# A one-core encoder layer in fp32: squares moved between engines at the start, SSD chunk outputs ahead of the next chunk, embedding product behind its gate

## The chip, the cores and the metric

The kernel runs on one core of a Trainium2 chip. The metric is device time in microseconds of one execution. The five engines are PE (TensorE, matmuls), DVE (VectorE), ACT (ScalarE), POOL (GpSimd) and SP (SyncE, which issues the DMAs here, strictly in order).

## The reference

One layer of a hybrid streaming encoder, for 512 prompt tokens and 32 sample tokens (T = 544 together), width 1024:

```
h = rmsnorm(x); q, k, v, z, xBC, dt, gates = split(h @ w_in)
ya = band_attention(rms(q), rms(k), v, rel_bias)          # 16 heads of 64, chunk band of 9 x 64 tokens
xs, B, C = split(silu(causal_dwconv(xBC)))                # 32 heads of 64 in 4 groups, state 128
y = chunked scan: per chunk  (C B^T * decay) @ (dt x) + C @ h * exp(acs);  h' = h * exp(last) + B^T @ wj
yb = rmsnorm((y + d_skip * xs) * silu(z))
x += (sigmoid(ga) * (ya @ w_proj_a) + sigmoid(gb) * (yb @ w_proj_b)) @ w_out
x += down(gelu(conv(ug)) * conv(uv))                      # u = rmsnorm(x) @ w_up
x += sigmoid(rmsnorm(x) @ w_ple_gate) * (p @ w_ple)
```

Outputs are x and the new caches and states. The sample tokens go through the same code with their own cached context.

## The kernel before

Activations lie transposed, 128 features by 544 tokens, in eight tiles. Every dense product is made from fp32 split into a high and a low part (`hi`, `lo` for activations, `wh`, `wl` for weights): `mm3` (L283) issues `wh*hi`, `wh*lo` and `wl*hi`, each for two halves of 272 tokens. This group of six matmuls is called a chunk below; a dense step has eight chunks (an embedding step `pw` only two) and ends with an epilogue that takes the result out of one of two PSUM buffers `dps`. The weights come as raw units of 128x1024 (`wr`, two per DMA, two DMAs' worth of buffers), are cast on ACT (L250) and their low part is made on DVE or, for odd early units, on POOL (L254).

The order of all dense steps is a list, `dense_steps` (L31). `dense.run(n)` works off n chunks of it, and the code of the other stages is written between such calls: this is what places SSD scan, attention and statistics between the dense matmuls on PE. The tile framework schedules each engine's instructions from this program order and puts in the semaphores; on an engine they then run in that order.

- **Beginning.** `Dense.start` (L334) runs the first two steps together while x is still arriving: `split_g` (L371) makes `hi` on ACT (L374) and `lo` on DVE (L375) for x[0] to x[7]. The squares of x are made on POOL for k = 0 to 3 (L443, added L445), on ACT for 4 to 7 (L380, L383), and summed on DVE (L384, L448) into `acc`. `rstd_of` (L392) multiplies `acc` by ones on PE (`rps`) and takes Ln (L404) and Exp (L409) on ACT. The `dt` product (`dtp`, L473) follows. Until `rstd` is there no epilogue can run.
- **Bias table.** `bias_vector` (L551) negates a small table (`er`, L554), copies it (`e0`, L555), writes both to DRAM (`evec`, L556, L557), from where 16 DMAs (`bsc`, L563, 320 KB each) spread it.
- **SSD scan** (loop L1139). Four groups of heads, in each the prompt chunks 0 to 3 and the sample chunk 4, which goes together with chunk 0 (a pair): 16 turns. `ssd_a` (L613) makes `cbt` and the transposes `xst` on PE, scales `dx` and `wj` on DVE (L637), loads `ab` by DMA (L645), and from it makes the decay `m` (relu L650, exp L655 on ACT, product L656 on DVE) and the scaled C (exp L659 on ACT, product L660 on POOL). `ssd_b` (L665) multiplies (`yps`), adds the outputs to `xs` on DVE (L690), makes the new state (`st` on PE, POOL L699, DVE L701, or an ACT copy L703 for chunk 0), and writes `out_o_hs` (L705) after chunk 4 and `out_o_hp` (L710) after chunk 3. A turn is `ssd_a(n)`, some dense chunks, `ssd_b(n-1)`, some dense chunks. `cbt`, `xst`, `yps` and `st` share four PSUM slots.
- **Attention.** Eight pairs of heads in blocks of 128 queries. `stack` (L816) prepares the keys and queries `ks`, `qs` of the next pair, `att_a` makes the logits `L`, `att_b` transposes the weights (`Tp`), `att_c` multiplies by v. `FILL` (L1157) holds for each block how many dense chunks stand before and behind `att_b`.
- **End.** After the last `down` step come eight `pw` steps, copied to SBUF by ACT (L1089), a second `rstd`, eight gate steps with tanh (`ep_final`, L1096), the last of them in two halves (`last_gate`, L1104).

## Time and profile before

| | |
|---|---|
| median of 3 runs (lowest, highest) | 1356.16 us (1355.61, 1357.16) |
| profiled execution | 1355.77 us |
| its span | 1354.1 us |
| mean granted clock of PE over the span | 0.999 |
| PE busy | 1338.2 us, 99% |
| DVE, ACT, POOL busy | 852.6, 634.4, 313.7 us |
| DMA | 142.15 MB, 106 GB/s over the span |

The span is the profiled part of the execution; the remaining 1.67 us lie around it. Busy times of engines overlap. In timelines, consecutive instructions of one kind are one row, whose duration goes from the first start to the last end.

### The profile page before, as it was taken

Reading aid. Unit: us, or ns where it says so; the run is one execution under the profiler, and the core shown is the slowest. Engines: PE = TensorE matmul, PEld = TensorE weight load, DVE = VectorE, ACT = ScalarE, POOL = GpSimd, SP = SyncE. Lnnn points to the kernel's source line nnn. Section 1 sums busy time; section 2 is a strip of 40 time slices with the busy share of each in tenths; the row PEclk is TensorE's granted clock in tenths of the full one; section 3 lists DMA queues with packets and bytes.
Section 4 is the critical chain, followed back from the end, with each engine's and each line's share of the span. In section 5 each row is a group of like instructions: output and inputs, shape, how many; then the busy total and the mean of one; then the engine's idle time right before and its main releaser. Section 6 shows DMA issues by size and latency. Waiting matters only on the chain.

```text
span 1354.1 us, 26563 instructions
## 1 busy us (share of the span) xinstructions
PE 1338.2 (99%) x11045; PEld 1307.2 (97%) x11045; DVE 852.6 (63%) x1474; ACT 634.4 (47%) x1104; POOL 313.7 (23%) x442
## 2 busy tenths in 40 slices
PE   8999999999999999999999999999999999999998
PEld 7999998999999999999999999999999999999998
DVE  7999889755775656643554335677676356753545
ACT  5465555656676667542442223534444124432342
POOL 5456365544321211100000000133332013310000
PEclk9999999999999999999999999999999999999999
DMA  5733243332533332222223422222222232222231
GB/s 182 252 100 130 83 128 121 119 132 100 177 94 114 115 111 90 67 81 94 69 89 110 143 94 73 85 94 94 94 72 85 94 111 94 76 85 94 94 107 53
DMA packets 41896, 142.15 MB, mean 105 GB/s; under 512 B 9216, under 2 KB 13232, under 8 KB 29488
## 3 DMA queue, kind: packets, MB, share of 16 engines
q1 hardware_dynamic: 41776, 140.45, 31.4%
q8 instruction: 87, 1.43, 0.4%
q14 instruction: 33, 0.27, 0.1%
HBM read 129.27 MB, written 14.31 MB: 106 GB/s over the span
## 4 chain that ended last, share of the span: by engine, by line
PE 89%; DVE 6%; ACT 2%; DMA 1%; issue 1%; SPq 0%; POOL 0%; ACTq 0%; DVEq 0%; POOLq 0%
PE dps L130 80%; PE O L130 2%; PE yps L130 2%; PE L L130 1%; PE st L130 1%; DVE cv L599 1%; DVE qs L834 1%; PE Tp L133 1%; DVE wl L254 1%; PE xst L133 0%; PE gps L130 0%; DMA wr<-in_w 0%; DVE xs L603 0%; DMA ab<-asc 0%; PE qn L130 0%
## 5 line engine op out<-in xcount | busy, mean ns | idle before, releaser
L130 PE MATMUL dps<-hi,wh 128*128 128x272 f32 x2960 | 627.0, 293 | 0.6 <-DVE ext L574 0.4
L130 PE MATMUL dps<-lo,wh 128*128 128x272 f32 x2960 | 613.1, 288 | 4.1 <-DVE lo L375 4.1
L130 PE MATMUL dps<-hi,wl 128*128 128x272 f32 x2960 | 612.1, 288 | 0.0
L130 PEld LDWEIGHTS dps<-hi,wh 128*128 128x128 f32 x2960 | 466.0, 189 | 10.5 <-issue 7.8
L130 PEld LDWEIGHTS dps<-lo,wh 128*128 128x128 f32 x2960 | 465.9, 189 | 5.0 <-DVE lo L375 5.0
L130 PEld LDWEIGHTS dps<-hi,wl 128*128 128x128 f32 x2960 | 464.9, 188 | 0.0
L250 ACT CAST wh<-wr 128x1024 fp32r<-128x1024 f32 x192 | 201.2, 1048 | 386.0 <-PE dps L130 346.6
L254 DVE TENSOR_TENSOR wl<-wr,wh 128x1024 fp32r<-128x1024 f32 x173 | 213.6, 1235 | 47.6 <-ACT wh L250 42.3
L1033 DVE SCALAR_TENSOR_TENSOR ucv<-uext,vec,ucv 128x546 f32<-128x546 f32 x96 | 75.3, 784 | 4.4 <-ACT ucv L1030 2.7
L599 DVE SCALAR_TENSOR_TENSOR cv<-ext,hv,cv 128x547 f32<-128x547 f32 x72 | 71.0, 986 | 2.1 <-ACT cv L596 1.0
L1026 POOL COPY cfo<-uext 128x2 f32<-128x2 f32 x48 | 10.4, 217 | 261.7 <-DVE uext L573 261.7
L1023 POOL MEMSET uext<- 128x2 f32 x48 | 4.5, 95 | 278.7 <-issue 278.7
L1065 DVE TENSOR_TENSOR x<-x,dps 128x544 f32<-128x544 f32 x24 | 17.3, 721 | 78.0 <-PE dps L130 78.0
L571 DVE TENSOR_TENSOR uext<-dps,rstd 128x272 f32<-128x272 f32 x48 | 21.3, 443 | 63.0 <-PE dps L130 58.3
L785 DVE CUSTOM_DVE_ANT_0 P<-L,bias 128x128 f32<-128x128 f32 (+3 forms) x64 | 30.8, 481 | 46.1 <-PE L L130 41.6
L254 POOL TENSOR_TENSOR wl<-wr,wh 128x1024 fp32r<-128x1024 f32 x19 | 48.4, 2549 | 43.9 <-ACT wh L250 42.4
L1027 POOL COPY cfo<-uext 128x2 f32<-128x2 f32 x48 | 55.5, 1157 | 0.0
L787 ACT ACTIVATE P<-P,sm 128x128 f32<-128x128 f32 (+3 forms) x64 | 36.0, 562 | 26.8 <-DVE sm L785 26.4
L660 POOL TENSOR_TENSOR ab<-ab,bc 128x512 f32<-128x512 f32 (+1 forms) x28 | 37.0, 1325 | 40.7 <-ACT ab L659 40.7
L368 ACT CAST hi<-me 128x544 fp32r<-128x544 f32 x24 | 15.5, 647 | 61.9 <-DVE me L1051 61.9
L1030 ACT ACTIVATE ucv<-uext,vec 128x546 f32<-128x546 f32 x48 | 40.7, 847 | 7.2 <-DVE uext L574 2.6
L650 ACT ACTIVATE m<-ab,tm 128x128 f32<-128x128 f32 x128 | 40.8, 389 | 6.3 <-DMA ab<-asc 6.2
(243 smaller groups left out, 1548.9 us busy)
## 6 DMA issues: line engine op xcount, KB each, us to landing
wr<-in_w SPq DMA_DIRECT2D x96, 1024.0 KB, 4.9
ab<-asc SPq DMA_DIRECT2D x32, 256.0 KB, 5.1
bsc<-evec SPq DMA_DIRECT2D x16, 320.0 KB, 8.0
bias<-bsc SPq DMA_DIRECT2D x16, 256.0 KB, 3.2
xin<-in_xT SPq DMA_DIRECT2D x8, 272.0 KB, 5.7
out_o_v<-v SPq DMA_DIRECT2D x8, 272.0 KB, 3.2
out_o_k<-qk SPq DMA_DIRECT2D x8, 272.0 KB, 2.9
x<-in_xT SPq DMA_DIRECT2D x8, 272.0 KB, 4.4
```

Source lines behind the costliest of these rows:

```text
L130: return self._pin(nc.tensor.matmul(*args, **kw))
L250: cp = S.copy(hi, r)
L254: eng.tensor_tensor(lo, r, hi.bitcast(F32), op=SUB)
L571: V.tensor_tensor(ext[:, n : n + HALF], ps[:, 0, :HALF], rstd[:, 0:HALF], op=MUL)
L599: V.scalar_tensor_tensor(y[:, :n], ext[:, j : j + n], hv[:, 24 * j + ti : 24 * j + ti + 1], y[:, :n], op0=MUL, op1=ADD)
L650: S.activation(m[:, i], ab[:Q, i], AF.Relu, scale=-1.0, bias=tm[:Q, 1, c, hd : hd + 1])
L660: G.tensor_tensor(ab, ab, cc[:, tk].unsqueeze(1).to_broadcast([128, H, Q]), op=MUL)
L785: V.tensor_tensor_reduce(out=P, in0=L, in1=B, scale=1.0, scalar=3e38, op0=ADD, op1=MIN, accum_out=nm[:n])
L787: S.activation(P, P, AF.Exp, scale=-1.0, bias=nm[:n], accum_out=sm[:n])
L1027: G.tensor_copy(cfo[:, i, 2:4], ext[:, UW - 2 : UW])
L1030: S.activation(y[:, :n], ext[:, 0:n], AF.Identity, scale=vec[:, V_FW + i : V_FW + i + 1], bias=vec[:, V_FB + i : V_FB + i + 1])
L1033: V.scalar_tensor_tensor(y[:, :n], ext[:, j : j + n], vec[:, V_FW + 48 * j + i : V_FW + 48 * j + i + 1], y[:, :n], op0=MUL, op1=ADD)
```

## The change

- The squares at the beginning: x[0] on ACT directly into `acc` behind the first weight parts, x[1] to x[5] on ACT behind the last split, x[6] and x[7] on POOL with their sum; DVE adds the six results behind the last `lo`. The load of `hb` goes out before that of the second weight pair.
- The `dt` product is cut in two halves, one before and one behind the statistics matmul.
- The table's negate is tied behind the last instruction of the dt softplus (`last_dt`), the copy follows it.
- In `rstd_of`, Ln and Exp stand in one loop.
- SSD: `ssd_b(n-1)` directly ahead of `ssd_a(n)`, then all dense chunks of the turn.
- `FILL`: block (even pair, 2) from (2, 3) to (3, 4), block (even pair, 3) from (2, 4) to (2, 2).
- End: gate steps first, the statistics six chunks behind the last `down`, tanh kept in eight tiles, then the `pw` steps, whose result DVE reads from PSUM; the last `pw` step in two halves.

```diff
-    p += [("pw", m) for m in range(8)] + [("gate", m) for m in range(8)]
+    p += [("gate", m) for m in range(8)] + [("pw", m) for m in range(8)]
...
+            dtp = [dt_product(0)]
             first_rstd.append(rstd_of(rstd, acc, 1.0 / D))
+            dtp.append(dt_product(1))
             for st, ps in zip(sts, pss):
                 epilogue[st[0]](ps, *st[1:])
-            dt_product()
+            dt_scale(dtp)
...
             ln = S.activation(dst[:, sl], ps[:, :HALF], AF.Ln, bias=eps, scale=scale)
...
-        for h in range(2):
-            sl = slice(h * HALF, (h + 1) * HALF)
             last = S.activation(dst[:, sl], dst[:, sl], AF.Exp, scale=-0.5)
...
+        if k == 0:
+            sq0 = S.activation(acc, xt[0], AF.Square)
+            tc.add_manual_dep(sq0.ins, last_part[0].ins.name, ORDER, reason="order")
+    nc.sync.dma_start(hb, a["hb"].unsqueeze(0).to_broadcast([128, 2, 32]))
     load(1)
-    nc.sync.dma_start(hb, a["hb"].unsqueeze(0).to_broadcast([128, 2, 32]))
...
-    acc2 = slot(name="acc2")
-    for k in range(KD):
-        if k < 4:
-            q = acc2 if k == 0 else eslot("sq")[:, :T]
-            G.tensor_tensor(q, xt[k], xt[k], op=MUL)
-            if k > 0:
-                G.tensor_tensor(acc2, acc2, q, op=ADD)
-        else:
-            if k == 6:
-                V.tensor_tensor(acc, acc, acc2, op=ADD)
-            add_sq(acc, xt[k], k == 4, V)
-    done(acc2)
+    q6, q7 = eslot("sq"), eslot("sq")
+    for q, k in ((q6, 6), (q7, 7)):
+        G.tensor_tensor(q[:, :T], xt[k], xt[k], op=MUL)
+    G.tensor_tensor(q6[:, :T], q6[:, :T], q7[:, :T], op=ADD)
+    for k in range(1, 6):
+        q = eslot("sq")
+        tc.add_manual_dep(S.activation(q[:, :T], xt[k], AF.Square).ins, last_split[0].ins.name, ORDER, reason="order")
+        tc.add_manual_dep(V.tensor_tensor(acc, acc, q[:, :T], op=ADD).ins, last_split[1].ins.name, ORDER,
+                          reason="order")
+    V.tensor_tensor(acc, acc, q6[:, :T], op=ADD)
...
-        V.tensor_scalar(er[0:16, 0:257], er[0:16, 0:257], -1.0, None, op0=MUL)
+        neg = V.tensor_scalar(er[0:16, 0:257], er[0:16, 0:257], -1.0, None, op0=MUL)
+        tc.add_manual_dep(neg.ins, last_dt[0].ins.name, ORDER, reason="order")
...
+            if m == 7:
+                sp2 = sum_parts(acc)
+                dense.defer(6, lambda: rstd_of(rstd, sp2, 1.0 / D, gelus))
...
     def ep_pw(ps, m):
-        t = slot(name="pw")
-        S.copy(h2(t), pv(ps))
-        pw.append(t)
...
+        t = pg[m]
+        V.scalar_tensor_tensor(h2(t), h2(t), 1.0, pv(ps), op0=ADD, op1=MUL)
+        V.scalar_tensor_tensor(x[m], t, 0.5, x[m], op0=MUL, op1=ADD)
         nc.sync.dma_start(a["o_y"][m], x[m])
...
-        nxt = [ssd_a(g, i) for i in ((4, 0), (1,), (2,), (3,))[c]]
-        fa, fb = ((10, 9), (8, 8), (8, 7), (8, 7))[c]
-        dense.run(fa)
         if prev is not None:
             ssd_b(prev)
-        prev = nxt
-        dense.run(fb)
+        prev = [ssd_a(g, i) for i in ((4, 0), (1,), (2,), (3,))[c]]
+        dense.run((19, 16, 15, 15)[c])
...
-    FILL = {(0, -1): (2, 2), (0, 0): (3, 1), (0, 1): (1, 3), (0, 2): (2, 3), (0, 3): (2, 4),
+    FILL = {(0, -1): (2, 2), (0, 0): (3, 1), (0, 1): (1, 3), (0, 2): (3, 4), (0, 3): (2, 2),
...
-    last_gate()
+    last_pw()
```

On DVE, at the beginning, behind the first three `lo`, the kernel before has (L375 is `lo`, L384 and L448 the additions of squares, `hv` small scalings of constants):

```order
L375 SCALAR_TENSOR_TENSOR lo<-xin,vec,hi 128x544 x3
L384 TENSOR_TENSOR acc<-acc,sq 128x544
L459 TENSOR_SCALAR hv<-vec 128x120
L460 TENSOR_SCALAR hv<-vec 128x16
L461 TENSOR_SCALAR hv<-vec 128x1
L375 SCALAR_TENSOR_TENSOR lo<-xin,vec,hi 128x544
L448 TENSOR_TENSOR acc<-acc,acc_200 128x544
L375 SCALAR_TENSOR_TENSOR lo<-xin,vec,hi 128x544
L384 TENSOR_TENSOR acc<-acc,sq 128x544 x2
L254 TENSOR_TENSOR wl<-wr,wh 128x1024
```

and the changed kernel (L380 is `lo`, L452 and L454 the additions):

```order
L380 SCALAR_TENSOR_TENSOR lo<-xin,vec,hi 128x544 x4
L463 TENSOR_SCALAR hv<-vec 128x120
L464 TENSOR_SCALAR hv<-vec 128x16
L465 TENSOR_SCALAR hv<-vec 128x1
L380 SCALAR_TENSOR_TENSOR lo<-xin,vec,hi 128x544
L452 TENSOR_TENSOR acc<-acc,sq 128x544 x5
L454 TENSOR_TENSOR acc<-acc,sq 128x544
L255 TENSOR_TENSOR wl<-wr,wh 128x1024
```

Four additions became six, and all stand behind the last `lo`. On SP, from the last copies of the bias table to the loads of the second SSD chunk, the kernel before has:

```order
L563 DMA bsc_254<-evec 128x640
L237 DMA wr<-in_w 128x2048 x2
L545 DMA asc<-dtx 32x4x128
L547 DMA asc<-dtx 32x32
L237 DMA wr<-in_w 128x2048
L645 DMA ab<-asc 128x8x32
L645 DMA ab<-asc 128x512 x2
L237 DMA wr<-in_w 128x2048
L645 DMA ab<-asc 128x512 x2
L237 DMA wr<-in_w 128x2048
L705 DMA out_o_hs<-h 128x512
L645 DMA ab<-asc 128x512 x2
```

and the changed kernel, where nine of the 16 `bsc` come behind `asc`:

```order
L553 DMA asc<-dtx 32x4x128
L555 DMA asc<-dtx 32x32
...
L572 DMA bsc_254<-evec 128x640
L238 DMA wr<-in_w 128x2048
L654 DMA ab<-asc 128x8x32
L654 DMA ab<-asc 128x512 x2
L238 DMA wr<-in_w 128x2048
L714 DMA out_o_hs<-h 128x512
L654 DMA ab<-asc 128x512 x2
L238 DMA wr<-in_w 128x2048
L654 DMA ab<-asc 128x512 x2
```

The `bsc` moved from ahead of two weight loads to directly ahead of the first `ab`, and the second pair of `ab` (chunk 1) from ahead of `out_o_hs` to behind it; the same exchange is found in all four groups. On DVE, at the first pair of the scan, the kernel before has (`m` of 32x256 is chunk 4, the two of 128x512 are chunk 0):

```order
L656 TENSOR_TENSOR m<-m,cbt 32x256
L599 SCALAR_TENSOR_TENSOR cv<-ext,hv,cv 128x547 x2
L656 TENSOR_TENSOR m<-m,cbt 128x512
L571 TENSOR_TENSOR ext<-dps,rstd 128x272
L573 TENSOR_TENSOR ext<-dps,rstd 128x240
L574 TENSOR_TENSOR ext<-dps,rstd 128x32
L603 SCALAR_TENSOR_TENSOR xs<-th,cv 128x512
L604 SCALAR_TENSOR_TENSOR xs<-th,cv 128x32
L656 TENSOR_TENSOR m<-m,cbt 128x512
```

and the changed kernel (L699 are the additions of the outputs, which read `yps`):

```order
L665 TENSOR_TENSOR m<-m,cbt 32x256
L608 SCALAR_TENSOR_TENSOR cv<-ext,hv,cv 128x547
L665 TENSOR_TENSOR m<-m,cbt 128x512
L580 TENSOR_TENSOR ext<-dps,rstd 128x272
L582 TENSOR_TENSOR ext<-dps,rstd 128x240
L583 TENSOR_TENSOR ext<-dps,rstd 128x32
L255 TENSOR_TENSOR wl<-wr,wh 128x1024
L699 SCALAR_TENSOR_TENSOR xs<-xs,vec,yps 128x32
L612 SCALAR_TENSOR_TENSOR xs<-th,cv 128x512
L613 SCALAR_TENSOR_TENSOR xs<-th,cv 128x32
L699 SCALAR_TENSOR_TENSOR xs<-xs,vec,yps 128x32 x3
L665 TENSOR_TENSOR m<-m,cbt 128x512
```

The second `m` of chunk 0 moved behind the output additions of chunk 4.

## Rows read from the trace of the kernel before

**Rows 1.** The page, part 1: busy us (share of the span) and instructions of each engine.

```profile
PE 1338.2 (99%) x11045; PEld 1307.2 (97%) x11045; DVE 852.6 (63%) x1474; ACT 634.4 (47%) x1104; POOL 313.7 (23%) x442
```

**Rows 2.** Waits of PE: waiting line <- releaser: us in total, times, longest.

```profile
PE dps L130 <- DVE lo L375: 4.1, 3, 3.3
PE st L130 <- DVE xs L690: 1.8, 2, 1.2
...
PE L L130 <- DMA ks<-ks: 1.0, 2, 0.8
...
PE L L130 <- ACT qs L752: 0.6, 1, 0.6
```

**Rows 3.** Windows: us, busy (instructions) of PE, PEld, DVE, ACT, POOL, clock, DMA.

```profile
0.00:20.00 20.00, 14.42 (x73) 13.05 (x74) 13.63 (x19) 11.68 (x20) 14.59 (x28) 0.91 0.89 301
...
80.00:160.00 80.00, 79.34 (x689) 75.06 (x688) 76.70 (x138) 48.67 (x102) 41.10 (x53) 1.00 0.35 111
...
600.00:620.00 20.00, 20.00 (x162) 20.00 (x161) 7.53 (x8) 7.34 (x8) 0.00 (x0) 1.00 0.32 106
```

**Rows 4.** Timeline of PE, beginning: start, duration, operation, count [idle before <- releaser].

```profile
16.15 0.55 PE L130 MATMUL dps<-lo,wh 128*128 128x272 f32 x2 [3.27 <-DVE lo L375]
...
25.07 1.08 PE L130 MATMUL rps<-acc,ones 128*128 128x272 f32 x4
...
28.56 0.49 PE L130 MATMUL dps<-hi,wh 128*128 128x272 f32 x2 [0.44 <-DVE ext L574]
```

**Rows 5.** Timeline of DVE, beginning.

```profile
10.97 3.35 DVE L260 TENSOR_TENSOR wl<-wr,wh 128x512 fp32r<-128x512 f32 x2
14.24 4.70 DVE L375 SCALAR_TENSOR_TENSOR lo<-xin,vec,hi 128x544 fp32r<-128x544 f32 x3
...
21.80 1.54 DVE L384 TENSOR_TENSOR acc<-acc,sq 128x544 f32<-128x544 f32 x2
```

**Rows 6.** Timeline of POOL, beginning.

```profile
10.43 1.84 POOL L445 TENSOR_TENSOR acc<-acc,sq 128x544 f32<-128x544 f32 x1
```

**Rows 7.** Timeline of DVE: the copy of the bias table and the last dt step.

```profile
28.34 2.58 DVE L555 COPY e<-er 16x383 f32<-16x383 f32 x1
...
55.52 0.31 DVE L512 SCALAR_TENSOR_TENSOR tm<-dtt 128x160 f32<-128x160 f32 x1
```

**Rows 8.** Timeline of SP's DMA issues, 30 to 102 us.

```profile
32.48 1.21 SPq L563 DMA_DIRECT2D bsc<-evec  x2
...
34.38 14.32 SPq L563 DMA_DIRECT2D bsc<-evec  x14
...
72.86 1.53 SPq L645 DMA_DIRECT2D ab<-asc  x3
...
101.91 0.34 SPq L705 DMA_DIRECT2D out_o_hs<-h  x1
```

**Rows 9.** The page, part 6: DMA issues, KB each, median us from issue to landing.

```profile
ab<-asc SPq DMA_DIRECT2D x32, 256.0 KB, 5.1
bsc<-evec SPq DMA_DIRECT2D x16, 320.0 KB, 8.0
bias<-bsc SPq DMA_DIRECT2D x16, 256.0 KB, 3.2
```

**Rows 10.** Timeline of PE: outputs of the first pair.

```profile
95.81 0.65 PE L130 MATMUL yps<-m,dx 32*64 32x32 f32 x16
```

**Rows 11.** Timeline of DVE: the second product of chunk 0 of the first group.

```profile
87.87 0.67 DVE L656 TENSOR_TENSOR m<-m,cbt 128x512 f32<-128x512 f32 x1
```

**Rows 12.** Timelines of ACT and POOL: from the first relu to the last product, chunk 1.

```profile
92.90 1.28 ACT L650 ACTIVATE m<-ab,tm 128x128 f32<-128x128 f32 x4 [0.28 <-DMA ab<-asc]
...
101.20 1.29 POOL L660 TENSOR_TENSOR ab<-ab,bc 128x512 f32<-128x512 f32 x1
```

**Rows 13.** Timeline of DVE at the last `down` step.

```profile
1288.42 0.72 DVE L1065 TENSOR_TENSOR x<-x,dps 128x544 f32<-128x544 f32 x1 [2.58 <-PE dps L130]
...
1292.70 0.73 DVE L389 TENSOR_TENSOR al<-acc,ah 128x544 fp32r<-128x544 f32 x1 [0.84 <-ACT ah L388]
```

More of the change, by code (lines that the diff above doesn't have):

```diff
@@ L228, in trunk @@
     raws = {0: r0}
+    last_part = []
     ready = {}
@@ L258, in prep_part @@
         hi, lo = ready[u]
-        S.copy(hi[:, c0:c1], r[:, c0:c1])
+        last_part[:] = [S.copy(hi[:, c0:c1], r[:, c0:c1])]
         V.tensor_tensor(lo[:, c0:c1], r[:, c0:c1], hi[:, c0:c1].bitcast(F32), op=SUB)
@@ L370, in split @@
         return hi, lo
+    last_split = []
     def split_g(x, g):
         hi, lo = slot(F32R, "hi"), slot(F32R, "lo")
-        S.activation(hi, x, AF.Copy, scale=g)
-        V.scalar_tensor_tensor(lo, x, g, hi.bitcast(F32), op0=MUL, op1=SUB)
+        last_split[:] = [S.activation(hi, x, AF.Copy, scale=g),
+                         V.scalar_tensor_tensor(lo, x, g, hi.bitcast(F32), op0=MUL, op1=SUB)]
         return hi, lo
@@ L471, in trunk, with dt_product, dt_scale @@
     bsc = [dram.tile([128, EROW], F32, name=f"bsc{h}", tag=f"bsc{h}") for h in range(16)]
-    def dt_product():
-        ps = [sps("dtp") for _ in range(2)]
-        for h in range(2):
-            for k in range(KD):
-                j = 32 * (k % 4)
-                PE.matmul(ps[h][j : j + 32, :HALF], lhsT=dtw[:, 32 * k : 32 * k + 32],
-                          rhs=xt[k][:, h * HALF : (h + 1) * HALF], start=k < 4, stop=k >= 4)
+    def dt_product(h):
+        ps = sps("dtp")
+        for k in range(KD):
+            j = 32 * (k % 4)
+            PE.matmul(ps[j : j + 32, :HALF], lhsT=dtw[:, 32 * k : 32 * k + 32],
+                      rhs=xt[k][:, h * HALF : (h + 1) * HALF], start=k < 4, stop=k >= 4)
+        return ps
+    last_dt = []
+    def dt_scale(ps):
         done(dtw_t, *xt)
@@ L511, in dt_softplus @@
         dt = tm[:, 0]
-        V.scalar_tensor_tensor(dt, p, 2.0, x, op0=MUL, op1=ADD)
+        last_dt.append(V.scalar_tensor_tensor(dt, p, 2.0, x, op0=MUL, op1=ADD))
         ea = const.tile([128, 32], F32, name="ea")
@@ L1075, in trunk @@
     ph = []
-    pw = []
+    pg = []
     def acts_pw(st):
@@ L1083, in acts_pw, with ep_final_gate @@
         return ph
-    parts = []
-    def ep_pw(ps, m):
-        t = slot(name="pw")
-        S.copy(h2(t), pv(ps))
-        pw.append(t)
-        if m == 0:
-            parts.append(sum_parts(acc))
-        if m == 7:
-            dense.defer(4, lambda: rstd_of(rstd, parts[0], 1.0 / D, gelus))
-    def ep_final(ps, m):
-        t = eslot("pg")
-        V.tensor_tensor(h2(t[:, :T]), pv(ps), h2(rstd), op=MUL)
-        S.activation(t[:, :T], t[:, :T], AF.Tanh, scale=0.5)
-        V.scalar_tensor_tensor(t[:, :T], t[:, :T], 1.0, pw[m], op0=ADD, op1=MUL)
-        V.scalar_tensor_tensor(x[m], t[:, :T], 0.5, x[m], op0=MUL, op1=ADD)
+    def ep_final_gate(ps, m):
+        t = slot(name="pg")
+        V.tensor_tensor(h2(t), pv(ps), h2(rstd), op=MUL)
+        S.activation(t, t, AF.Tanh, scale=0.5)
+        pg.append(t)
@@ L1102, in ep_final, with last_pw @@
+    def ep_pw(ps, m):
+        t = pg[m]
+        V.scalar_tensor_tensor(h2(t), h2(t), 1.0, pv(ps), op0=ADD, op1=MUL)
+        V.scalar_tensor_tensor(x[m], t, 0.5, x[m], op0=MUL, op1=ADD)
         nc.sync.dma_start(a["o_y"][m], x[m])
-    def last_gate():
-        t, m = eslot("pg"), 7
+    def last_pw():
+        m = 7
+        t = pg[m]
         pss = [sps("gps") for _ in range(2)]
-        w = next_unit(*units_of(("gate", m))[0])
+        ws = [tuple(w[:, 768 + 128 * j : 896 + 128 * j] for w in pw_w["w"]) for j in range(2)]
@@ L1108, in last_gate @@
         for h in range(2):
             sl = slice(h * HALF, (h + 1) * HALF)
-            for n in range(KD):
-                wh, wl = (v[:, 128 * n : 128 * n + 128] for v in w)
-                for i, (l, r) in enumerate(((wh, xp[n][0]), (wh, xp[n][1]), (wl, xp[n][0]))):
+            for n, (wh, wl) in enumerate(ws):
+                for i, (l, r) in enumerate(((wh, ph[n][0]), (wh, ph[n][1]), (wl, ph[n][0]))):
                     PE.matmul(pss[h][:, :HALF], lhsT=l, rhs=r[:, sl], start=n == i == 0,
-                              stop=n == KD - 1 and i == 2)
@@ L1115, in last_gate @@
-            V.tensor_tensor(t[:, sl], pss[h][:, :HALF], rstd[:, sl], op=MUL)
-            S.activation(t[:, sl], t[:, sl], AF.Tanh, scale=0.5)
-            V.scalar_tensor_tensor(t[:, sl], t[:, sl], 1.0, pw[m][:, sl], op0=ADD, op1=MUL)
+                              stop=n == 1 and i == 2)
+            V.scalar_tensor_tensor(t[:, sl], t[:, sl], 1.0, pss[h][:, :HALF], op0=ADD, op1=MUL)
             V.scalar_tensor_tensor(x[m][:, sl], t[:, sl], 0.5, x[m][:, sl], op0=MUL, op1=ADD)
@@ L1132, in trunk @@
         "pa": ep_pa, "pb": ep_pb, "out": ep_out, "ug": ep_ug, "uv": ep_uv, "down": ep_down,
-        "pw": ep_pw, "gate": ep_final,
+        "pw": ep_pw, "gate": ep_final_gate,
     })
```

## Prediction

> **What bounds the kernel now.** I read the page's first part, the waits of PE, the windows, then the timelines of the stretches that the diff touches. PE is busy for 1338.2 of 1354.1 us [rows 1], and the four waits on other engines that the change touches make 7.5 us [rows 2]: it can win a few of these, and it can lose by a new one. In the undisturbed middle PE does 162 matmuls of 128x272 in 20 us [rows 3], 0.124 us each, so a dense chunk (six of them) is 0.74 us and a step of eight chunks 6 us. In the first 20 us the granted clock is 0.91 [rows 3]: part of that time runs at 1.2 GHz instead of 2.4. The profiled execution took 1355.77 us, 1.67 of it around the span, 0.39 below the median of the runs; the sum is made against 1355.8, and 0.4 is added at the end. About 0.2% (2.7 us) is what a measurement of this kernel can tell from no change.
>
> **1. Beginning.** PE waited 3.27 us for the fourth `lo` and went on at 16.15. The 58 dense matmuls from there to the statistics matmul at 25.07 take 8.92 us where 58 x 0.124 = 7.2 would do [rows 4], so this wait also cost 1.7 us of clock. The `lo` was late because POOL squared and added beside DVE. From 10.97 to 18.94 DVE did two half `wl` and three `lo` [rows 5]; an addition of the same 128x544 takes 0.77 when uncrowded (two in 1.54 [rows 5]), so the five need about 2 x 0.72 + 3 x 0.77 = 3.75 alone. The other 4.2 us went to four POOL instructions, one of which shows 1.84 us [rows 6]: 1.05 each. After the change POOL is quiet until x[6] is there, so the fourth `lo` comes near 12.9, and PE loses neither the 3.27 nor the clock: its matmuls end near 20.1, the first half of the dt product 1 us later. But now the statistics matmul waits for DVE. From 10.97 DVE has the two `wl` (1.45), five `lo` (3.85), six additions that follow each other (4.6) and three POOL instructions beside it (3.15), 13.1 us and a few small scalings: 24.3. The matmul starts there instead of at 25.07, and the 3.49 us from it to the next dense matmul stay [rows 4]: **-0.8**. Ends: -4.0 (25.07 - 21.1, if POOL cost DVE nothing) and +0.9 (the new wait of 3.2 us is as long as the old one, and the clock falls again for 1.7 us). I take -0.8, because the 1.05 comes from the same two engines in the same stretch. The Trainium skill, "TensorE: Matmul & The Clock Gate", section "HAM oscillation — how this bites in real kernels", warns that a matmul stream with long waits goes back to the half clock after each; by that rule it is +0.9.
>
> **2. SSD loop, what goes.** Today `st` waits 1.8 us for the output additions [rows 2]; in the new order other matmuls stand there. **-1.8** (0 to -1.8).
>
> **3. SSD loop, first pair.** Today the bias table's copy ran on DVE at 28.34 and the 16 `bsc` copies went out from 32.48 [rows 7, 8], 4.1 us later. Now both table steps are pinned behind the last dt step, which ran at 55.52 [rows 7], so the `bsc` begin near 60. All 16 took 16.2 us to issue (32.48 to 48.70) [rows 8], and each lands 8.0 us after its issue [rows 9]. In the new order of SP the first `ab` loads stand behind them all: issue at about 76.5, against 72.86 today [rows 8], and with the burst's tail still in flight they land 3.5 to 6.5 us later than now. Meanwhile PE wants this pair's `yps` earlier: they began at 95.81 [rows 10], with eight chunks and one `cbt`/`xst` block (6.0 + 0.7) more ahead of them than in the new order, so now at 95.81 - 6.7 - 0.8 = 88.3, and the last four heads of chunk 0, some 1.6 into the block, at 89.9. Their `m` product ran on DVE from 87.87 to 88.5 [rows 11]. With the loads late it ends at 91.2 to 94.2, since DVE's queue also has it behind an addition of chunk 4 that waits for `yps` itself. PE waits 1.3 to 4.3: **+3.0** (0 to +7, if the loads wait out the whole 8.0 of the last `bsc`).
>
> **4. SSD loop, chunk 1 of each group.** SP issues `ab` of chunk 1 now after `out_o_hs`, which waits for the state `h` of chunk 4; today it went out before. `out_o_hs` was issued 101.91 - 95.81 = 6.1 us after the pair's `yps` began [rows 8, 10]; the first `ab` load follows 0.4 later and lands 5.1 on [rows 9], at 11.6. From the first relu on that load to the end of POOL's second product it is 102.49 - 92.90 = 9.6 us today [rows 12], an estimated 2.3 of it for other work in between; so the product stands at 18.9 to 21.2. PE gets there after `yps` (2.1), two `st` (2.2), `cbt`/`xst` (0.7), 16 chunks (11.9) and half of the new `yps` (1.0): 17.9. That is a wait of 1.0 to 3.3 per group; nearer the lower end, since ACT and POOL are not full, 1.25, four times: **+5.0** (0 to +13). It is nothing if the load lands as the `bias` load of the same size does, in 3.2 us [rows 9]. The Trainium skill, "DMA: Bandwidth & Descriptors", section "Anatomy of one DMA — SWDGE (gpsimd) path", fits a DMA as 2.0 us plus its bytes at 436 GB/s, an estimated 2.6 us for these 256 KB; the row has 5.1, and I keep the row.
>
> **5. SSD loop, slots.** `yps`, `st`, `cbt` and `xst` now come in a row out of four PSUM slots, and where a pair comes in there are six: the fifth and sixth wait for DVE's four additions and for `h`. The nearest row is the 0.9 that each of the two waits of `st` took [rows 2]; I take a third of it at three places, **+1.0** (0 to +3).
>
> **6. Attention.** The `L` matmuls that wait for `ks` (1.0) and `qs` (0.6) [rows 2] get two more chunks (1.5 us) ahead of them, so these waits go. The two chunks are taken from behind the transposes of the pair's last block, where two (1.5 us) still cover one copy: **-1.6** (-1.6 to +0.5).
>
> **7. End.** The second statistics matmul comes six chunks after the last `down`, which DVE takes from PSUM at 1288.42: 1288.4 + 4.5 = 1292.9, while `al` ends at 1292.70 + 0.73 = 1293.4 [rows 13]: +0.5. Behind the last matmul stand two DVE instructions instead of a product, a tanh and these two: -0.9, of which the last steps, paced by two DVE instructions of 0.72 each (as the `x` addition [rows 13]) against 1.5 us of PE, give back 0.4. **0** (-0.9 to +0.9). The Ln/Exp loop is merged in the code, but ACT's order stays: nothing.
>
> Sum: -0.8 - 1.8 + 3.0 + 5.0 + 1.0 - 1.6 + 0 = +4.8, so 1360.6 on the profiled execution and **1361.0** as a median.
>
> **The rivals.** *The cover holds* (faster): the loads of chunk 1 land in 3.2 us, and terms 3 to 5 shrink to +1 together. With term 1 between -0.8 and -4.0 the sum is -3.2 to -6.4: about 1351.5. For it: 16 chunks of cover are 12 us, nearly what the chain needs. Against: DVE is busy for 76.7 of the 80 us from 80 to 160 [rows 3] and has no room to be early. It decides at 17.9 us from the pair's `yps` to POOL's product. *It cancels* (no difference): the lower ends of terms 3 and 4 (1.3 and 4 x 0.3) with -4.2 elsewhere, 1355 to 1357. By the DMA figure that the Trainium skill gives (quoted in 4), term 4 would be 0 and this the case. *The clock falls as well* (slower still): term 1 at +0.9 instead of -0.8, 1362.7. For it: the old wait of 3.27 did it [rows 4]; against: no shorter wait in the trace did. That the change does not do what it says is so for the Ln/Exp merge alone, which has no price.
>
> **How the numbers follow.** Forecast 0.37, the clock falls as well 0.13: both slower, 0.50. Cancels: 0.22. Cover holds: 0.28. The forecast's own range is 1359 to 1368, the top where term 4 costs 3 us per group. To hold eight in ten the range reaches into the faster case: 1351 to 1368. Faster by over 0.2% 0.28, within 0.22, slower 0.50.
>
> **What would show it.** Right: a wait of PE's statistics matmul for DVE's additions of some 3 us between 21 and 25, and none for `lo`; `yps` among PE's waits, for `m` in the first pair and for POOL's `ab` in chunk 1 of the groups; `bsc` issued from 60 to 76; the waits of `L` gone. Wrong: `yps` waits for less than 3 us in all, or the first dense matmul behind the statistics stands 2 us or more earlier than 28.56.

## The result and the profile after

The changed kernel took **1371.34 us** in the median (six runs, 1369.92 to 1372.21) against 1356.65 (1355.48 to 1362.03) of the kernel before on the same chip: ratio **1.0103** (95% interval 1.0085 to 1.012), 14.7 us slower. That is outside the predicted range (1351 to 1368): the direction was right, the predicted loss of 4.8 us a third of the real one. The profiled execution has a span of 1370.5 us, 16.4 more than before.

The page of the changed kernel, part 1 (as [rows 1]):

```profile
PE 1346.0 (98%) x11045; PEld 1308.7 (95%) x11045; DVE 849.5 (62%) x1475; ACT 632.9 (46%) x1097; POOL 310.0 (23%) x438
```

PE has the same 11045 instructions as before and is busy for 7.8 us more (1346.0 to 1338.2), and it is idle for 8.6 us more (1370.5 - 1346.0 = 24.5 to 15.9). The mean granted clock over the span is 0.994, before 0.999, and the windows below show where it is lower: of the 16.4 us, about half is waiting and half is clock. The table of PE's waits of the changed kernel says where it was idle (as [rows 2]: us in total, times, longest):

```profile
PE yps L130 <- DVE m L665: 5.2, 2, 3.2
PE cbt L130 <- DVE xs L699: 3.5, 2, 2.4
PE yps L130 <- POOL ab L669: 2.7, 2, 2.5
PE rps L130 <- DVE acc L454: 2.2, 1, 2.2
...
PE qn L130 <- POOL ql L750: 1.1, 1, 1.1
...
PE dps L130 <- DVE lo L380: 0.8, 3, 0.3
...
PE L L130 <- DMA ks<-ks: 0.4, 1, 0.4
```

The waits of `st` are gone, those for `lo` are down from 4.1 us to 0.8 and those of `L` from 1.6 to 0.4; in their place stand three kinds of waits in the scan, one at the statistics and one for POOL ahead of the attention. The windows of the changed kernel (as [rows 3]) say where the clock was:

```profile
0.00:20.00 20.00, 16.96 (x108) 15.38 (x109) 13.18 (x20) 12.50 (x22) 7.89 (x22) 1.00 0.86 280
20.00:40.00 20.00, 17.54 (x139) 14.50 (x139) 17.43 (x32) 10.97 (x16) 5.50 (x13) 0.91 0.22 79
...
80.00:100.00 20.00, 14.72 (x121) 11.76 (x120) 15.76 (x35) 9.74 (x20) 7.19 (x10) 0.83 0.50 155
100.00:120.00 20.00, 20.00 (x158) 18.68 (x157) 13.38 (x26) 10.45 (x21) 9.24 (x11) 0.91 0.36 119
...
220.00:240.00 20.00, 17.63 (x141) 17.26 (x141) 17.81 (x38) 10.47 (x22) 7.87 (x14) 0.91 0.35 109
```

Before, of these only the first 20 us stood below 1.00 (0.91 [rows 3], where 80 to 160 is at 1.00). Two more windows of the kernel before:

```profile
20.00:40.00 20.00, 19.56 (x170) 17.96 (x169) 17.11 (x32) 9.41 (x14) 4.88 (x9) 1.00 0.30 94
...
220.00:240.00 20.00, 18.84 (x172) 17.20 (x171) 19.11 (x36) 12.30 (x23) 9.10 (x10) 1.00 0.40 125
```

The first 20 us are now at 1.00, and part of the time from 20 to 40, from 80 to 120 and from 220 to 240 runs at 1.2 GHz instead of 2.4, each time right behind the waits.

Where the two kernels drift apart, read at the same matmul of PE in both (time after minus time before):

| place | before | after | lag |
|---|---|---|---|
| first `cbt` of the scan | 73.10 | 72.59 | -0.5 |
| behind the first pair's block, equal matmuls done | 106.79 | 114.98 | +8.2 |
| ahead of chunk 3 of group 1, equal matmuls done | 197.43 | 208.25 | +10.8 |
| behind chunk 3 of group 1 and the pair's block, equal matmuls done | 221.59 | 239.40 | +17.8 |
| first `L` of the attention | 354.21 | 372.55 | +18.3 |
| last `L` | 574.38 | 590.37 | +16.0 |
| end of the span | 1354.1 | 1370.5 | +16.4 |

So the beginning wins half a us, the scan loses 18.8, the attention wins 2.4, the end loses 0.4. Most of the loss stands at two places: 8.7 us at the first pair and 7.0 at chunk 3 of group 1. Another 2.6 lie between them, behind shorter waits at the change from group 0 to group 1 (0.22 for POOL's `ab`, 1.16 for DVE's additions).

**The first pair.** SP's DMA issues of the changed kernel (as [rows 8]):

```profile
59.82 4.88 SPq L572 DMA_DIRECT2D bsc<-evec  x7
...
67.53 8.64 SPq L572 DMA_DIRECT2D bsc<-evec  x9
...
76.85 5.56 SPq L654 DMA_DIRECT2D ab<-asc  x3
...
99.63 0.34 SPq L714 DMA_DIRECT2D out_o_hs<-h  x1
100.02 0.91 SPq L654 DMA_DIRECT2D ab<-asc  x2
```

The three `ab` issues begin four us later than before (76.85 to 72.86) and take 5.56 us instead of 1.53 [rows 8]. DVE's timeline shows when the first of them is there, and what DVE does until the last product of chunk 0 is made (as [rows 11]; start, duration, operation, count, idle before it):

```profile
86.76 0.41 DVE L661 TENSOR_TENSOR m<-ab,tm 32x256 f32<-32x256 f32 x1 [3.32 <-DMA ab<-asc]
...
91.20 0.67 DVE L665 TENSOR_TENSOR m<-m,cbt 128x512 f32<-128x512 f32 x1
...
92.56 1.20 DVE L255 TENSOR_TENSOR wl<-wr,wh 128x1024 fp32r<-128x1024 f32 x1
...
94.56 0.55 DVE L699 SCALAR_TENSOR_TENSOR xs<-xs,vec,yps 128x32 f32<-128x32 f32 x3
95.03 0.67 DVE L665 TENSOR_TENSOR m<-m,cbt 128x512 f32<-128x512 f32 x1
```

and PE's timeline shows what that costs (as [rows 10]):

```profile
90.62 0.65 PE L130 MATMUL yps<-m,dx 32*64 32x32 f32 x16 [2.05 <-DVE m L665]
...
95.75 1.12 PE L130 MATMUL yps<-m,dx 128*64 128x128 f32 x8 [3.17 <-DVE m L665]
96.81 4.08 PE L130 MATMUL st<-wj,bt 32*128 32x512 f32 x4
```

Two waits, 5.2 us together, and behind them four `st` in 4.08 us, where two take 1.1 at the full clock. DVE stood idle for 3.32 us until the load came, and then had all the work of this turn to do at once; the second `m` is made 7.2 us later than before (95.03 to 87.87 [rows 11]).

**Chunk 3 of group 1.** Timelines of POOL, PE and DVE of the changed kernel, 213 to 224 us:

```profile
213.14 2.38 POOL L255 TENSOR_TENSOR wl<-wr,wh 128x1024 fp32r<-128x1024 f32 x1 [0.61 <-POOL cso L602]
215.47 1.75 POOL L669 TENSOR_TENSOR ab<-ab,bc 128x512 f32<-128x512 f32 x1
```

```profile
217.28 0.44 PE L130 MATMUL yps<-ab,h 128*64 128x128 f32 x4 [2.47 <-POOL ab L669]
...
222.41 0.46 PE L130 MATMUL cbt<-bc 128*128 128x128 f32 x2 [2.37 <-DVE xs L699]
```

```profile
214.82 3.81 DVE L608 SCALAR_TENSOR_TENSOR cv<-ext,hv,cv 128x547 f32<-128x547 f32 x3 [0.57 <-ACT cv L605]
218.54 1.22 DVE L255 TENSOR_TENSOR wl<-wr,wh 128x1024 fp32r<-128x1024 f32 x1
...
221.15 1.11 DVE L699 SCALAR_TENSOR_TENSOR xs<-xs,vec,yps 128x128 f32<-128x128 f32 x4
```

No load is late here. POOL has a weight's low part (2.38 us) ahead of the product that `yps` needs; and DVE comes to the output additions at 221.15, though `yps` was complete near 218.1, since three convolution steps, a low part and an epilogue stand ahead of them. The second `cbt` of the pair gets its PSUM slot only when these additions have read it. The old loop had the `cbt` block of the pair first, then ten dense chunks (7.4 us), then the `yps` block, and nine more chunks ahead of the second `cbt`; now nothing stands between them.

### The profile page after: what moved, and what is told of

It reads as the page before. It is cut to its first block, busy times and chain, and to the rows that moved or that the text cites. A ratio compares the mean times of both kernels' runs of the same rounds, so it can differ in the third digit from the quotient of the medians.

```text
span 1370.5 us, 26551 instructions
## 1 busy us (share of the span) xinstructions
PE 1346.0 (98%) x11045; PEld 1308.7 (95%) x11045; DVE 849.5 (62%) x1475; ACT 632.9 (46%) x1097; POOL 310.0 (23%) x438
## 4 chain that ended last, share of the span: by engine, by line
PE 83%; DVE 8%; ACT 3%; DMA 3%; issue 1%; POOL 1%; SPq 0%; DVEq 0%; ACTq 0%; POOLq 0%
PE dps L130 74%; DVE cv L608 2%; PE O L130 2%; DMA ab<-asc 2%; PE L L130 2%; PE yps L130 1%; PE Tp L133 1%; PE st L130 1%; DVE wl L255 1%; ACT m L659 1%; ACT wh L251 1%; DVE qs L843 1%; DVE xs L699 1%; PE qn L130 0%; DMA xin<-in_xT 0%
## 5 line engine op out<-in xcount | busy, mean ns | idle before, releaser
L580 DVE TENSOR_TENSOR uext<-dps,rstd 128x272 f32<-128x272 f32 x48 | 21.2, 442 | 63.6 <-PE dps L130 58.8
L669 POOL TENSOR_TENSOR ab<-ab,bc 128x512 f32<-128x512 f32 (+1 forms) x28 | 40.7, 1455 | 34.2 <-ACT ab L668 33.7
```

What stands on the lines that cost most here:

```text
L580: V.tensor_tensor(ext[:, n : n + HALF], ps[:, 0, :HALF], rstd[:, 0:HALF], op=MUL)
L669: G.tensor_tensor(ab, ab, cc[:, tk].unsqueeze(1).to_broadcast([128, H, Q]), op=MUL)
```

## Experiments

Each ran beside the kernel before; the differences below are of medians against it, on the same chip.

**Which part costs it.** Four kernels: the change without the order between the table and the dt softplus; the change with the old loop; the new loop alone in the kernel before; the order alone in the kernel before. The two edits are:

```diff
-        neg = V.tensor_scalar(er[0:16, 0:257], er[0:16, 0:257], -1.0, None, op0=MUL)
-        tc.add_manual_dep(neg.ins, last_dt[0].ins.name, ORDER, reason="order")
+        V.tensor_scalar(er[0:16, 0:257], er[0:16, 0:257], -1.0, None, op0=MUL)
```

```diff
+        nxt = [ssd_a(g, i) for i in ((4, 0), (1,), (2,), (3,))[c]]
+        fa, fb = ((10, 9), (8, 8), (8, 7), (8, 7))[c]
+        dense.run(fa)
         if prev is not None:
             ssd_b(prev)
-        prev = [ssd_a(g, i) for i in ((4, 0), (1,), (2,), (3,))[c]]
-        dense.run((19, 16, 15, 15)[c])
+        prev = nxt
+        dense.run(fb)
```

> The changed kernel with one part undone: the table's negate is no longer tied behind the last dt step, so the 16 bsc copies go out near 32 us again. Both together (the late copies delay the first ab loads just where the new loop order wants the first pair's yps 7 us earlier): the 8.7 us lost at the first pair go down to 1 at most, the 7.0 at the second pair change stays, about 1363. Loop order alone: the wait of the first pair stays, about 1370. Pin alone: all that was lost comes back, about 1355.

> The changed kernel with the SSD loop of before (ssd_a, half the chunks, ssd_b, the other half), the pin kept. Both together: yps of the first pair have their eight chunks more ahead of them, so the late loads cost 0 to 3, and the waits of cbt go; 1353 to 1356. Loop order alone: the same or a little better, about 1353. Pin alone: the first pair still loses 8, about 1362.

> The kernel before with the new SSD loop alone. Both together: first pair without its wait (m of chunk 0 stands ahead of the output additions again), the waits of cbt and of yps at the changes of group stay (9 us less the 1.8 of st): about 1364. Loop order alone: first pair 8.7 and changes of group 9: about 1372. Pin alone: no change from before, 1356 to 1357.

> The kernel before with the pin alone. Both together: the bsc copies at 60 to 76 us delay the first ab loads by 7 to 9 us, but yps of the first pair stand at 95.8 as before: 0 to 3 us, about 1358. Loop order alone: no change, 1356.5. Pin alone: about 1364.

Measured: without the order 1365.38 (+8.6, ratio 1.0065, 1.0046 to 1.0085); with the old loop 1357.95 (+1.1, ratio 1.0006, 0.9991 to 1.002); the new loop alone 1369.61 (+12.8, ratio 1.0097, 1.0077 to 1.0117); the order alone 1362.2 (+5.4, ratio 1.0035, 1.0018 to 1.0051). The parts cost what they cost by themselves, so theories in which only both together do harm fell. The order costs in the old loop too, where it shows as another wait. PE's timeline of the changed kernel with the old loop:

```profile
97.25 1.12 PE L130 MATMUL st<-wj,bt 32*128 32x512 f32 x2
102.63 2.05 PE L130 MATMUL st<-wj,bt 128*128 128x512 f32 x2 [4.26 <-DVE xs L699]
```

The second pair of `st` waits 4.26 and then runs at half the clock (2.05 for two, 1.12 above it).

**Both undone**, with the beginning, attention and end as changed:

> The changed kernel with the old SSD loop and without the order between the bias table and the dt softplus; beginning, attention and end stay changed. If the parts add, the time is that of the changed kernel less what the two undone parts cost (13 and 6 us): 1352.5, or 4 below the kernel before, PE still waiting 2.2 us for DVE's additions of squares near 22, the two waits of st at 0.9 each, no wait of L. The rival (the table's order only costs because something else of the changed kernel is early, so without the loop nothing is left to win) gives 1356 to 1358, the level of the run with the old loop and the order kept.

1351.98 (-4.3, ratio 0.9968, 0.9957 to 0.9979): the parts add, since each costs about the same with the others and without them. The new loop costs 8.6 + 4.3 = 12.9 here and 12.8 alone, the order 14.7 - 8.6 = 6.1 and 5.4, and the rest wins 4.3: 12.9 + 6.1 - 4.3 = 14.7. By the profiles the loop's 12.4 us of span (1363.1 to 1350.7) are 6.3 of PE being busy longer (1343.2 to 1336.9) and 6.1 of idle time. From the first `cbt` to the first `L` alone, where the two kernels differ, it is 12.8 us (293.5 to 280.7), 5.6 of PE being busy longer and 7.2 of idle time.

**What in the loop costs it.** First, the dense chunks put elsewhere (no order of the table):

```diff
+        nxt = [ssd_a(g, i) for i in ((4, 0), (1,), (2,), (3,))[c]]
+        dense.run(4)
         if prev is not None:
             ssd_b(prev)
-        prev = [ssd_a(g, i) for i in ((4, 0), (1,), (2,), (3,))[c]]
-        dense.run((19, 16, 15, 15)[c])
+        prev = nxt
+        dense.run((15, 12, 11, 11)[c])
```

> The changed kernel without the table's order, its loop now ssd_a(n), four chunks, ssd_b(n-1), the rest of the chunks. From cbt of a chunk to its yps stand 20 dense chunks of two turns instead of 16 (24 before), and yps, st and the next cbt no longer follow each other. Theory (the new loop costs because cover of some 6 us is taken from the way from ab to m, and because cbt of the next chunk needs a PSUM slot that DVE has only just emptied): both kinds of waits go, 1353 to 1356, and the windows after the first 40 us show 1.00. Rival (what costs is the moved place of the loads and additions on SP and DVE, whatever stands on PE): 1360 to 1365, waits of yps for ab of 2 us or more stay.

```diff
             ssd_b(prev)
+        dense.run(2)
         prev = [ssd_a(g, i) for i in ((4, 0), (1,), (2,), (3,))[c]]
-        dense.run((19, 16, 15, 15)[c])
+        dense.run((17, 14, 13, 13)[c])
```

> The changed kernel without the table's order, two dense chunks (1.5 us) taken from behind ssd_a and put between ssd_b(n-1) and ssd_a(n); it stands against the run without the table's order (1365.4, waits of cbt 2.9, of yps for ab 3.9). Theory (two separate waits: cbt for an emptied PSUM slot, yps for a product that is late by its chain): waits of cbt fall from 2.9 to under 1, waits of yps for POOL's ab stay or grow by up to 1.5 at each of the places, so 1363 to 1367. Rival (both have one cause, DVE's additions being late in its queue): both fall together and the time comes under 1362.

Four between: 1361.61 (+5.3, ratio 1.0039, 1.0025 to 1.0053), the rival's figure, but by waits that neither theory named; two ahead: 1358.92 (+2.6, ratio 1.0017, 1.0006 to 1.0027), where both kinds of waits fell, as the rival with one cause had it, and the waits of `yps` moved from POOL's product to DVE's. Four against eight chunks between the blocks are 9.6 us. The waits of PE, first of the kernel with four between, then of that with two ahead:

```profile
PE st L130 <- DVE wj L645: 4.2, 3, 2.4
PE yps L130 <- DVE wj L645: 3.1, 2, 2.2
```

```profile
PE yps L130 <- DVE m L664: 2.8, 4, 1.9
...
PE cbt L130 <- DVE xs L698: 0.4, 1, 0.4
```

With four between, `yps` does not wait for its own inputs but for `wj` of the next chunk, which empties the PSUM slot of `xst`: four chunks are 3 us, and DVE comes to it later than that. So in each of these orders PE waits for DVE or POOL. That DVE, or POOL, is short of time at these places was then put to the test by taking work off them. The low parts of the weight units 8 to 39 were left out (even units on DVE, odd units on POOL); their third product takes `wh` for `wl`, so these units' outputs are another product, at the same count and shape on PE:

```diff
+        skip = 8 <= u < 40 and u % 2 == 0
-        lo = wp.tile([128, 1024], F32R, tag="wl", name="wl", bufs=2)
+        lo = hi if skip else wp.tile([128, 1024], F32R, tag="wl", name="wl", bufs=2)
...
-        eng.tensor_tensor(lo, r, hi.bitcast(F32), op=SUB)
+        if not skip:
+            eng.tensor_tensor(lo, r, hi.bitcast(F32), op=SUB)
```

> The changed kernel without the table's order (1365.4, waits of cbt 2.9 and of yps for POOL 3.9), and DVE makes no low part wl for the even weight units 8 to 38; the third product of these units takes wh in its place, so PE's work is the same in number and shape. Theory (DVE's queue, 71 of 80 us busy from 80 to 160 in the run without the table's order, is what makes cbt wait): 16 instructions of 1.2 to 2.4 us less, cbt's waits fall under 0.7 in all, those of yps for POOL stay at 2 to 4: 1360 to 1363. Rival 1 (DVE's queue makes everything late, POOL's product too): both go, 1354 to 1356. Rival 2 (it is the order of PE's own work, no engine being short): both stay, 1364 to 1366.

> The same with POOL's wl of the odd units 9 to 39 left out, DVE's kept. Theory (POOL's wl of 2.4 us stands ahead of the product that yps waits for, and shares the time of DVE's instructions beside it): the waits of yps for POOL fall from 3.9 to under 1, and some of cbt's with them, 1358 to 1361. Rival (the product is late because ab and the exp on ACT are late): the waits of yps stay at 3 or more, 1363 to 1366.

> The changed kernel without the table's order, and the low parts of the units 8 to 39 left out on both engines (each third product takes wh in its place, PE's work stays the same in number and shape). Left out on DVE alone it came from 1365.4 to 1357.7, on POOL alone to 1356.9; with the old loop and both kept it is 1352.0. Theory (the new loop costs because DVE and POOL are late in their queues, and nothing else): with both gone no wait over 0.5 is left in the scan, 1351.5 to 1353. Rival (what is left of some 5 us is the order itself: cbt directly behind yps and st needs the slot that DVE has yet to empty, however free DVE is): waits of cbt of 1 to 2 stay, 1355 to 1357.

Without DVE's 1357.72 (+1.0, ratio 1.001, 1.0001 to 1.0019), without POOL's 1356.93 (+0.2, ratio 1.0001, 0.9991 to 1.0011), without both 1353.76 (-2.9, ratio 0.9978, 0.9967 to 0.9989). The waits, of the kernel without the order first, then of these three (the last has no wait of `yps` or `cbt` over 0.2):

```profile
PE yps L130 <- POOL ab L668: 3.9, 2, 2.5
PE cbt L130 <- DVE xs L698: 2.9, 4, 1.2
```

```profile
PE cbt L130 <- DVE xs L700: 2.2, 2, 1.4
...
PE yps L130 <- POOL ab L670: 0.4, 1, 0.4
```

```profile
PE cbt L130 <- DVE xs L700: 2.0, 1, 2.0
```

```profile
PE xst L133 <- DVE h L711: 0.6, 1, 0.6
```

Without POOL's low parts the waits went as the theory had it, and the time fell further. Without DVE's it was the other way round: the wait for POOL's product went, and 2.2 of `cbt` stayed. Either engine's relief helps the other. With both gone the new loop comes to 1.4 us above the old one with its low parts (-2.9 to -4.3), a little over the theory's figure and below the rival's. From the first `cbt` to the first `L` it takes 281.6 us, the old loop with its low parts 280.7 (1.8 of it idle) and the new loop with them 293.5. So the same order of PE's blocks is nearly free once DVE and POOL keep up: most of the cost is in their queues. The old loop without low parts was not run; by its idle time it could win an estimated 1.8 us, so the order itself may cost up to some 3.

The edit has a side effect, which no run takes out: without POOL's low parts, SP also issues the first `ab` load of chunk 3 of group 1 18.7 us ahead of its `yps` (184.80 to 203.45) instead of 15.3 (192.81 to 208.11 in the kernel without the order). There this is not what helped, since the load had landed 3 us or more ahead of ACT's relu in both (191.3 to 194.65, and 198.4 to 201.41). From this relu to the end of POOL's second product it is 8.6 us with POOL relieved and 10.4 without.

That POOL's work also slows DVE is in the rows. The convolution steps of DVE from 60 to 320 us (busy us, mean ns), without the order and then without POOL's low parts as well:

```profile
L607 DVE SCALAR_TENSOR_TENSOR cv<-ext,hv,cv 128x547 f32<-128x547 f32 x56 | 55.0, 981 | 10.8 <-ACT cv L604 10.1
```

```profile
L609 DVE SCALAR_TENSOR_TENSOR cv<-ext,hv,cv 128x547 f32<-128x547 f32 x57 | 49.7, 872 | 7.6 <-ACT cv L606 6.7
```

The same instruction is 109 ns shorter in the mean. The Trainium skill, "SBUF — State Buffer", section "SBUF: two separate sides", has DVE and GpSimd share a pair of ports that one of them holds for a whole instruction; the rows agree with that, though none shows the ports themselves.

**What in the order costs it.** The 16 copies of the table issued two at a time behind the `ab` loads of chunks 1 to 8, with the old loop, and in the changed kernel whole:

```diff
     def bias_rows(h):
-        nc.sync.dma_start(bsc[h], evec[h].unsqueeze(0).to_broadcast([128, EROW]))
+        row = nc.sync.dma_start(bsc[h], evec[h].unsqueeze(0).to_broadcast([128, EROW]))
+        tc.add_manual_dep(row.ins, last_ab[-1].ins.name, ORDER, reason="order")
...
+        for h in range(2 * n - 2, 2 * n) if 1 <= n <= 8 else ():
+            bias_rows(h)
```

> The changed kernel with the old loop and the table's order kept (1357.95 without this edit, one wait of st of 4.3 and the half clock after it), and the 16 copies of the bias table issued two at a time behind the ab loads of chunks 1 to 8. Theory (the order costs because 16 us of issues stand ahead of the first ab load on SP): the first ab loads go out at 73 and land by 79, the wait of st goes back to 0.9 twice, 1352 to 1353, the level of the run with neither. Rival (the negate and the copy, moved on DVE, are what makes DVE late): 1357 to 1358, the wait of st stays over 3.

> The changed kernel whole (new loop and the table's order), only the 16 copies of the table issued two at a time behind the ab loads of chunks 1 to 8. With the old loop this edit won back 3.6 of the 6.0 that the order cost. Theory (the loads of the first pair, late behind the copies, are most of the price here too): the waits of yps for m in the first pair (5.2) go, 1366 to 1367.5, the level of the run without the order (1365.4) and up to 2 above. Rival (in the new loop the negate and the copy on DVE, or the copies among the later loads, cost as much): 1369 to 1371.

In the changed kernel: 1364.8 (+8.2, ratio 1.006, 1.0044 to 1.0075), the level of the kernel without the order (+8.6). The 5.2 us of waits for `m` are down to

```profile
PE yps L130 <- DVE m L665: 1.0, 1, 1.0
```

so there the order's price, within the 0.6 us between these two, was that its copies stand ahead of the first `ab` loads. With the old loop: 1354.32 (-2.4, ratio 0.9981, 0.997 to 0.9992), between the theories, 1.9 above the kernel with neither (-2.4 to -4.3). The first wait of `st` is short again, but the other one of the two, at 230 us, is 1.8 instead of 1.0. Why is open.

**The attention alone.**

```diff
-    FILL = {(0, -1): (2, 2), (0, 0): (3, 1), (0, 1): (1, 3), (0, 2): (2, 3), (0, 3): (2, 4),
+    FILL = {(0, -1): (2, 2), (0, 0): (3, 1), (0, 1): (1, 3), (0, 2): (3, 4), (0, 3): (2, 2),
```

> The kernel before with the two moved chunks of the attention and nothing else. The prediction had -1.6 for it. Theory (the waits of L for ks and qs, 1.6, and of Tp for sm, 0.5, go): the matmuls from the first L to the last take 2 to 2.7 us less, 1353.5 to 1354.5. Rival (the gain comes from what the rest of the changed kernel does ahead of it): less than 1 us, 1355.5 to 1356.5.

1354.26 (-2.4, ratio 0.9977, 0.9968 to 0.9987). From the first `L` to the last (356.00 to 573.59, before 354.21 to 574.38) it is 2.6 us shorter, and the waits for `ks`, `qs` and `sm` are gone.

**The beginning, and a version that beats both.** From the kernel with neither: all squares on ACT, then DVE's `wl` of the third unit ordered behind the last addition.

```diff
-    q6, q7 = eslot("sq"), eslot("sq")
-    for q, k in ((q6, 6), (q7, 7)):
-        G.tensor_tensor(q[:, :T], xt[k], xt[k], op=MUL)
-    G.tensor_tensor(q6[:, :T], q6[:, :T], q7[:, :T], op=ADD)
-    for k in range(1, 6):
-        q = eslot("sq")
+    sq7 = slot(name="sq7")
+    for k in range(1, 8):
+        q = eslot("sq") if k < 7 else sq7
...
-    V.tensor_tensor(acc, acc, q6[:, :T], op=ADD)
+    done(sq7)
```

> As the first kernel of this call (old loop, no order of the table), and the squares of x[6] and x[7] and their sum taken from POOL too: all eight squares on ACT, seven additions on DVE. The price of a POOL instruction beside DVE was put at 1.05 us. If that holds, three of them less give 3.15 us to DVE and one addition more costs 0.77: the statistics matmul waits 2.4 us less than 2.2 for acc, so not at all, and the time falls by about 2 us against that kernel. Rival (in the changed kernel POOL lies beside DVE only while DVE waits for x anyway, or the DVE queue waits for the last square of ACT): the wait stays at 1.5 to 3 us and the time within 1 us.

```diff
-        eng.tensor_tensor(lo, r, hi.bitcast(F32), op=SUB)
+        sub = eng.tensor_tensor(lo, r, hi.bitcast(F32), op=SUB)
+        if u == 2:
+            tc.add_manual_dep(sub.ins, last_add.ins.name, ORDER, reason="order")
```

> The run with all squares on ACT (1350.84), and on DVE the low part wl of the third weight unit ordered behind the last addition of squares instead of ahead of it. There the wl took 1.22 us between the sixth addition and the seventh, and the statistics matmul waited 1.40. If the wl is what is left of the wait: matmul at 21.8 instead of 22.98, wait 0.2, 1349.6 to 1350. Rival (the third unit is then late for PE, which needs its wl soon after the statistics, or ACT's cast of the fourth unit ends last anyway): the gain at the statistics is given back behind it, 1350.5 to 1351.

Squares on ACT: 1350.84 (-5.4, ratio 0.996, 0.9946 to 0.9974), 1.1 below the kernel with neither, where 2 were expected for the price of POOL: the wait for `acc` went from 2.2 to 1.4 only, because a `wl` of 1.22 us lay between the last two additions. With that behind them: **1349.64** (-7.1, ratio 0.9946, 0.9932 to 0.9961), as expected. PE's timeline of this fastest kernel:

```profile
25.17 0.49 PE L130 MATMUL dps<-hi,wh 128*128 128x272 f32 x2 [1.17 <-ACT wh L251]
```

The first dense matmul behind the statistics stands 3.4 us earlier than before (25.17 to 28.56 [rows 4]). What it waits for now is a cast on ACT.

## Why the prediction was wrong, by its own steps

- **Term 1, beginning (-0.8): right.** The statistics matmul was put at 24.3 behind a new wait for `acc`; it started at 24.13, and the next dense matmul 0.8 earlier than before (27.79 to 28.56), of which 0.5 is left at the first `cbt`. PE's timeline of the changed kernel:

```profile
24.13 1.43 PE L130 MATMUL rps<-acc,ones 128*128 128x272 f32 x4 [2.21 <-DVE acc L454]
...
27.79 0.57 PE L130 MATMUL dps<-hi,wh 128*128 128x272 f32 x1 [0.25 <-ACT wh L251]
```

  The rival *the clock falls as well* came true here (0.91 from 20 to 40), and cost next to nothing: in the kernel with neither, whose clock stayed at 1.00, the next dense matmul also comes 3.4 us behind the statistics (24.49 to 27.90; here 3.66), since PE waits for ACT there.
- **Term 2 (-1.8): right.** The two waits of `st` are gone.
- **Term 3, first pair (+3.0, 0 to +7): right in mechanism, too small.** The issue was put at 76.5 and came at 76.85. But the first load landed at 86.7, 8.6 us later than before (78.2) and not 3.5 to 6.5, and PE waited twice (2.05 for chunk 4's `m`, 3.17 for chunk 0's) where one wait of 1.3 to 4.3 was reckoned. From -0.5 to +8.2 the pair cost 8.7: 5.2 of it are the two waits, and the other 3.5 are the clock, for which the sum had no term.
- **Term 4, chunk 1 of each group (+5.0): wrong.** No `yps` of a chunk 1 waits. SP issued the first load right behind `out_o_hs`, as reckoned (in group 2 only the second load: the first went out at 235.59, `out_o_hs` at 244.40, so the exchange is not the same in all four groups). But ACT has it 3.2 us later in group 0 (100.02 to 103.25), and it lands after 3.4 and 4.3 in groups 1 and 3, where 5.1 were taken; this is what the rival *the cover holds* said of it. From the pair's `yps` to the end of POOL's second product it is 18.0, 15.4 and 17.2 us in groups 1 to 3, where 18.9 to 21.2 were reckoned against a limit of 17.9. In group 0 it is 22.8 (90.62 to 113.46), but PE, itself late behind its two waits and the clock, comes only after 24.3 (114.91). Timelines of ACT and POOL in group 0, as [rows 12]:

```profile
103.25 1.28 ACT L659 ACTIVATE m<-ab,tm 128x128 f32<-128x128 f32 x4 [1.09 <-DMA ab<-asc]
```

```profile
111.68 1.78 POOL L669 TENSOR_TENSOR ab<-ab,bc 128x512 f32<-128x512 f32 x1
```

  The wait of this kind came at chunk 3 of group 1, where POOL's low part stood ahead of the product. The rival *it cancels* takes 0.3 per group as the lower end of this term, where the term itself has 1.0. The fit of the Trainium skill that the term quotes ("DMA: Bandwidth & Descriptors", section "Anatomy of one DMA — SWDGE (gpsimd) path") is for DMAs that GpSimd issues. SP issues these, and none of this size landed in less than 3.2 us in the changed kernel, where the estimate was 2.6.
- **Term 5, slots (+1.0, 0 to +3): the term that was most mis-sized.** It was taken as a third of 0.9 at three places. The two waits of `cbt` for the additions are 3.5 alone, and with the wait of `yps` at the same place and the clock behind both, the lag grows by some 7 us around chunk 3 of group 1. The prediction had the number that speaks of it, DVE busy for 76.7 of 80 us, and used it only as an argument against a rival. Terms 3 to 5 together, 9.0 by the sum, are the 18.8 that the scan lost plus the 1.8 of term 2, 20.6.
- **Term 6, attention (-1.6): right, a little small.** -2.4, and -2.6 in the profile of the two chunks alone: the wait for `sm` (0.5) went too.
- **Term 7, end (0): right.** +0.4: the statistics matmul waits 0.4 for `al`, as reckoned (0.5).
- **The step that failed** is the price of a wait in the scan. The sum counted a wait as its length: terms 2 to 5 are +7.2 us of waiting and nothing else. Measured from the first `cbt` to the first `L`, PE was idle for 12.9 us instead of 2.1, +10.7, and busy for 8.1 longer with the same work, for which no term stood. That the new waits by themselves (5.2 + 2.7 of `yps` and 3.5 of `cbt`, 11.4) come near terms 3 to 5 (9.0) is luck: the 5.0 of term 4 did not come, and the other two terms had 4.0. Across the whole kernel the clock added 7.8 us to 8.6 of idle time. The clock stood in the text as a rival for the beginning alone, with the argument that no shorter wait than 3.27 had done it; before, no wait between 1.3 and 3.2 was there to show it. The Trainium skill's rule quoted there ("TensorE: Matmul & The Clock Gate", section "HAM oscillation — how this bites in real kernels") was weighed at the one place where it cost nothing. In the scan of the changed kernel this case agrees with it: behind the waits of 2.05 and 3.17 the clock is 0.83 and 0.91. But the waits of that section's example are some 3 to 5 us long, mostly longer than these, and not every wait here was followed by a lower clock (see the last section). With neither the loop nor the order the windows from 80 to 280 show 1.00, the first of them:

```profile
80.00:160.00 80.00, 79.55 (x691) 75.28 (x690) 76.66 (x139) 47.91 (x99) 40.56 (x53) 1.00 0.34 111
```
